# A PSUM tile of its own for the chain of partial results in the FFN pairs with seven products

## The chip, the cores and the metric

The kernel runs on one core of a Trainium2 chip, in one launch. The metric is the device time of that core in microseconds. Before the change it is 1598.57 us, the median of three runs (1598.28 to 1598.74).

## What is computed

One layer of a hybrid streaming encoder is run for 256 prompt frames and 64 sample frames, in float32. The two groups share all weights, so the kernel treats them as one block of T = 320 columns. The reference, cut to the layer:

```python
def layer(x, ...):
    xn = rmsnorm(x, norm_mix[l])
    proj = xn @ w_in[l]                      # q, k, v, u, vs, gates
    ...                                      # attention, spatial gate, merge
    h = x + merged @ w_out[l]
    hn = rmsnorm(h, norm_ffn[l])
    gu = hn @ w_gate_up[l]                   # D_MODEL 2048 -> 2 * 5632
    h = h + (jax.nn.silu(gu[..., :D_FF]) * gu[..., D_FF:]) @ w_down[l]
    return h, k, v, vs
```

The change lies in `hn @ w_gate_up`.

## The kernel before

**Numbers.** A float32 operand is split into a high and a low float16 part (`half` for activations at L168, `high` at L373 and `low` at L377 for weights). A product is then three matmuls into the same PSUM columns: high by high, high by low, low by high (`product`, L104 to L110).

**Tiling.** The FFN has 44 column blocks of 128 features in gate and 44 in up. One group handles a block's gate (unit 0) and its up (unit 1), with 16 blocks along D_MODEL. In an ordinary group (`Group.block`) each unit is 16 times `product`, 48 matmuls of 128x320, into one `acc` tile. ScalarE reads that tile afterwards, in `gated` at L1173 and L1175.

**Pairs with seven products.** In 28 groups (class `Fast`, called pairs here) only high by high is done over all of D_MODEL and all 320 columns (`whole`, L419, 16 matmuls of 128x320 for each unit). The two correction terms are done together for gate and up and for both halves of the columns (N = 160) by a scheme of seven half-size products instead of eight (`cross`, L425, each 16 matmuls of 128x160). It needs four sums of weight parts (`sum_up`, L415, VectorE) and mixed activations (`mix`, made once). In the order in which TensorE does them in a pair, with the tile before the change:

| step | matmuls | tile |
|---|---|---|
| chain, first product (factor 11) | 16 of 160 columns | `more`, columns 0 to 159 |
| whole gate | 16 of 320 | `gate` |
| whole up | 16 of 320 | `up` |
| product 4 | 16 of 160 | `up` |
| chain, second product (factor 2) | 16 of 160 | `more`, columns 0 to 159 |
| product 21 | 16 of 160 | `gate` |
| other (factor 1, with the first sum), first half | 8 of 160 | `more`, columns 160 to 319 |
| row spread for a later group's scale (L222) | 1 of 128 | `row` |
| other, second half | 8 of 160 | `more`, columns 160 to 319 |
| third (factor 3, with the third sum) | 16 of 160 | `more`, columns 320 to 479 |
| product 22 (with the fourth sum) | 16 of 160 | `gate` |

The chain holds partial results that are wanted twice. ScalarE copies it to SBUF after its first product (`seen[:, 0]`, L436) and after its second (`seen[:, 1]`, L437). VectorE puts the pair together in `join` (L457 to L461), one pair later: L457 reads `gate` and `seen`, L458 and L461 read `other`, L459 reads `third`, L460 reads `up`. L1180 multiplies the result, and ScalarE takes its sum of magnitudes (L210).

**Tiles.** A PSUM tile is one bank. `acc` tiles have three banks, `aux` tiles four, `row` one. A new tile takes the bank of that kind that has been free longest, when its first instruction is placed. Before the change a pair takes one `acc` (`gate`) and two `aux` (`up`, `more`). A wait for data or for a bank is kept by whole tile: an instruction that writes into a tile waits for the last reader of it on another engine, whichever columns that reader took.

**Order.** Each engine works through its instructions in the order in which they are written down. Work is written at ticks (`at(tick, fn, rank)`): a pair has four ticks, an ordinary unit two, and what is due at a tick is written in the order of its rank, ahead of the matmuls that follow. A pair's weights are loaded 11 ticks ahead (five `raw` buffers), measured by ScalarE (`bound`, L210), turned into float16 high parts by ScalarE (L375) and low parts by VectorE (L378) into three `w` buffers. L1173 of an ordinary group and L1188 of a down block (`downed`) read a block's `acc` tile one tick after the block has ended. The copies L436 and L437 have rank 0.8 and so come first in their tick; `high` and `gated` have rank 2.

The 28 pairs come in three runs of 8, 12 and 8. In the profile of before they start at 822.97, 1081.89 and 1365.16 us. An ordinary up group stands ahead of the first run, down blocks ahead of the two others.

Of the kernel before, what the change touches and what calls it, by code (L numbers as in the profile page):

```python
# [51 lines left out]
def stream_step(ctx: ExitStack, tc: tile.TileContext, xT, w_in, w_a, w_b, w_out, w_gu, w_down,  # L52
# [10 lines left out]
    def acc():  # L63
        return psum.tile([P, 512], F32, tag="acc", bufs=3, name="acc")

    def aux():
        return psum.tile([P, 512], F32, tag="aux", bufs=4, name="aux")
# [8 lines left out]
    def at(tick, fn, *a, rank=5):  # L76
        if tick <= state["tick"]:
            fn(*a)
        else:
            later.setdefault(tick, []).append((rank, fn, a))  # L80

    def tick():
        state["tick"] += 1
        for _, fn, a in sorted(later.pop(state["tick"], ()), key=lambda x: x[0]):
            fn(*a)
# [305 lines left out]
    class Fast(Group):  # L391
# [35 lines left out]

        def blocks(self, x):
            assert state["tick"] == self.start
            gate, up, more = acc(), aux(), aux()  # L430
            part = lambda ps, n: ps[:, n * N : (n + 1) * N]
            turn_of["seen"] = turn_of.get("seen", 0) + 1
            self.seen = tmp.tile([P, 2, N], F32, tag="seen" if turn_of["seen"] % 2 else "sq", bufs=1, name="seen")
            self.chain, self.other, self.third = (part(more, n) for n in range(3))
            w0, w1, s, mid = self.w[0][2], self.w[1][2], self.sums, HALF // 2
            at(self.start + 1, lambda: nc.scalar.copy(out=self.seen[:, 0], in_=self.chain), rank=0.8)  # L436
            at(self.start + 3, lambda: nc.scalar.copy(out=self.seen[:, 1], in_=self.chain), rank=0.8)  # L437
            self.cross(self.chain, w0, 0, x, 11, start=True, stop=True)
            self.whole(gate, 0, x)
            tick()  # L440
            self.whole(up, 1, x)
            self.cross(part(up, 0), w1, HALF, x, 4, stop=True)
            self.cross(self.chain, s[2], 0, x, 2, stop=True)
            tick()
            self.cross(part(gate, 0), w0, HALF, x, 21)
            self.cross(self.other, s[1], 0, x, 1, range(0, mid), start=True)
            tick()
            self.cross(self.other, s[1], 0, x, 1, range(mid, HALF), stop=True)
            self.cross(self.third, s[3], 0, x, 3, start=True, stop=True)
            self.cross(part(gate, 1), s[4], 0, x, 22, stop=True)  # L450
            tick()
            return gate[:, :T], up[:, :T]
# [41 lines left out]
    first = [[acc(), acc()], [aux(), aux()], [aux(), aux()]]  # L494
# [429 lines left out]
    gate = {}  # L924
# [168 lines left out]
    for made, (kind, s, i) in enumerate(order):  # L1093
        s0, n = SLICES[s]
# [271 lines left out]
```

## Time and profile before

| | |
|---|---|
| median of three runs | 1598.57 us (1598.28 to 1598.74) |
| the profiled execution | 1598.67 us |
| its span, first to last instruction | 1596.9 us |
| TensorE (PE) busy | 1570.6 us, 98% of the span |
| VectorE (DVE) busy | 1214.8 us, 76% |
| ScalarE (ACT) busy | 1115.0 us, 70% |
| granted TensorE clock | 0.998 |
| weights and other data read | 256.03 MB, at 164 GB/s over the span |

A row of the timeline has the start in us, the duration in us, the engine, the line, the operation, the tiles written and read, the shape, and how many such instructions the row holds; in brackets stands how long the engine was idle just ahead of it and what ended that. PE is TensorE's matmul, PEld its weight load. Matmuls are pipelined: a row's duration runs to the modelled end of its last matmul, so the next row starts a little ahead of that end. A row of the groups of lines ends with the idle time ahead of those instructions and what released them. In the chain of waits each share is a part of the span.

### The profile page before, as it was taken

What the parts mean: (1) busy time and instruction counts of PE and PEld (TensorE: products, weight loads), DVE (VectorE), ACT (ScalarE), POOL (GpSimd) and SP (SyncE); (2) the same over time, 40 slices, a digit from 0 to 9 for tenths busy, and PEclk for the clock granted to TensorE, in tenths of its full rate; (3) what the DMA queues carried; (4) which work ended last, traced back from release to release, by engine and by line L of the source; (5) the groups of instructions that cost most, each with busy time, mean ns of one, the idle gap of its engine ahead of it and who ended that gap; (6) DMA issues with size and microseconds to landing.
All of it is one profiled execution on the core that took longest, in us unless ns stands there. A gap on an engine that the chain in (4) does not pass through costs nothing.

```text
span 1596.9 us, 31274 instructions
## 1 busy us (share of the span) xinstructions
PE 1570.6 (98%) x13047; PEld 1244.0 (78%) x13047; DVE 1214.8 (76%) x2109; ACT 1115.0 (70%) x1319; POOL 67.8 (4%) x80
## 2 busy tenths in 40 slices
PE   9999999999999999999999999999999999999997
PEld 9987777777777768879778877778888777888775
DVE  7789887977777766966969956549999655898675
ACT  6589888867556654846777778666777875677663
POOL 0110111100000000121000000000000000000000
PEclk9999999999999999999999999999999999999999
DMA  8567765654444444554554454543444544444441
GB/s 304 200 201 220 198 173 147 190 167 159 159 159 158 160 141 162 185 178 167 187 183 159 160 166 159 167 169 137 180 171 159 174 161 158 159 159 166 125 133 67
DMA packets 92462, 268.55 MB, mean 168 GB/s; under 512 B 28096, under 2 KB 34496, under 8 KB 85152
## 3 DMA queue, kind: packets, MB, share of 16 engines
q1 hardware_dynamic: 89872, 261.36, 49.3%
q0 software_dynamic: 1312, 3.80, 0.7%
q8 instruction: 102, 1.67, 0.4%
q10 hardware_dynamic: 1136, 1.39, 0.3%
q14 instruction: 40, 0.33, 0.1%
HBM read 256.03 MB, written 5.51 MB: 164 GB/s over the span
## 4 chain that ended last, share of the span: by engine, by line
PE 90%; ACT 6%; DVE 3%; issue 2%; DMA 0%; POOL 0%; DVEq 0%; ACTq 0%
PE acc L108 21%; PE acc L110 21%; PE acc L109 21%; PE aux L425 10%; PE acc L425 4%; PE aux L419 4%; PE acc L419 4%; PE aux L541 2%; ACT w L375 1%; PE acc L541 1%; DVE w L378 1%; ACT junk L210 1%; DVE tops L206 1%; ACT seen L437 1%; PE row L222 0%
## 5 line engine op out<-in xcount | busy, mean ns | idle before, releaser
L110 PE MATMUL acc<-half,w 128*128 128x320 f16 x2496 | 746.3, 299 | 1.2 <-DVE w L378 1.1
L108 PE MATMUL acc<-half,w 128*128 128x320 f16 x2496 | 746.4, 299 | 0.4 <-DVE gate L1056 0.3
L109 PE MATMUL acc<-half,w 128*128 128x320 f16 x2496 | 746.3, 299 | 0.0
L375 ACT ACTIVATE w<-raw,up 128x2048 f16<-128x2048 f32 (+1 forms) x216 | 425.1, 1969 | 274.6 <-PE acc L110 172.4
L378 DVE SCALAR_TENSOR_TENSOR w<-raw,up,w 128x2048 f16<-128x2048 f32 (+1 forms) x216 | 499.0, 2311 | 112.1 <-ACT w L375 111.8
L210 ACT ACTIVATE junk<-raw 128x2048 uint8<-128x2048 f32 (+1 forms) x190 | 354.6, 1866 | 6.7 <-issue 1.7
L108 PEld LDWEIGHTS <-w 128*128 128x128 f16 x2496 | 244.2, 98 | 97.6 <-issue 3.0
L110 PEld LDWEIGHTS <-w 128*128 128x128 f16 x2496 | 244.2, 98 | 96.5 <-DVE w L378 1.8
L109 PEld LDWEIGHTS <-w 128*128 128x128 f16 x2496 | 244.2, 98 | 90.8 <-issue 0.9
L226 DVE TENSOR_REDUCE peak<-row 128x1 f32<-128x128 f32 x159 | 45.7, 287 | 127.9 <-PE row L222 127.9
L425 PEld LDWEIGHTS <-sum 128*128 128x128 f16 x1792 | 126.9, 98 | 12.9 <-issue 12.9
L425 PE MATMUL aux<-mix,sum 128*128 128x160 f16 x1344 | 106.6, 232 | 9.4 <-ACT seen L437 9.4
L419 PEld LDWEIGHTS <-w 128*128 128x128 f16 x896 | 86.9, 98 | 31.9
L425 PEld LDWEIGHTS <-w 128*128 128x128 f16 x1344 | 96.2, 98 | 2.4
L415 DVE TENSOR_TENSOR sum<-w,sum 128x2048 f16<-128x2048 f16 x56 | 68.4, 1221 | 2.7
L415 DVE TENSOR_TENSOR sum<-w 128x2048 f16<-128x2048 f16 x56 | 68.2, 1217 | 0.0
L130 ACT CAST w<-raw 128x1024 fp32r<-128x1024 f32 x36 | 37.6, 1045 | 43.3 <-PE acc L110 29.5
L419 PE MATMUL acc<-half,w 128*128 128x320 f16 x448 | 65.4, 299 | 0.0
L419 PE MATMUL aux<-half,w 128*128 128x320 f16 x448 | 65.4, 299 | 0.0
L206 DVE TENSOR_REDUCE tops<-raw 128x1 f32<-128x2048 f32 x26 | 59.2, 2277 | 0.0
L210 ACT ACTIVATE junk<-act 128x320 uint8<-128x320 f32 x42 | 19.6, 467 | 50.4 <-DVE act L1180 41.5
L133 DVE TENSOR_TENSOR w<-raw,w 128x1024 fp32r<-128x1024 f32 x36 | 44.4, 1236 | 5.3 <-ACT w L130 5.2
(258 smaller groups left out, 1716.6 us busy)
## 6 DMA issues: line engine op xcount, KB each, us to landing
raw<-w_in SPq DMA_DIRECT2D x141, 512.0 KB, 4.8
raw<-w_gu SPq DMA_DIRECT2D x56, 1024.0 KB, 4.8
raw<-w_down SPq DMA_DIRECT2D x80, 512.0 KB, 4.0
raw<-w_gu SPq DMA_DIRECT2D x64, 512.0 KB, 4.8
raw<-w_out SPq DMA_DIRECT2D x32, 512.0 KB, 4.9
raw<-w_a SPq DMA_DIRECT2D x16, 512.0 KB, 3.5
raw<-w_b SPq DMA_DIRECT2D x16, 512.0 KB, 4.4
raw<-w_down SPq DMA_DIRECT2D x16, 256.0 KB, 4.1
```

The lines of the kernel that those rows point to most:

```text
L108: nc.tensor.matmul(ps[:, :T], a, x[0], start=first, stop=False, skip_group_check=True)
L109: nc.tensor.matmul(ps[:, :T], a, x[1], start=False, stop=False, skip_group_check=True)
L110: nc.tensor.matmul(ps[:, :T], b, x[0], start=False, stop=last, skip_group_check=True)
L206: nc.vector.tensor_reduce(out=self.tops[:, i : i + 1], in_=src, axis=mybir.AxisListType.X, op=ALU.max, apply_absolute_value=True)
L210: nc.scalar.activation(out=junk, in_=src, func=AF.Abs, accum_out=self.tops[:, i : i + 1])
L226: nc.vector.tensor_reduce(out=top, in_=self.row[:, :P], axis=mybir.AxisListType.X, op=ALU.max)
L375: nc.scalar.activation(out=w[:, 0], in_=self.raw[u][:, : self.width[u]], func=AF.Copy, scale=self.scale.up)
L378: nc.vector.scalar_tensor_tensor(out=self.w[u][1], in0=self.raw.pop(u)[:, : self.width[u]], scalar=self.scale.up, in1=self.w[u][0], op0=AL ...
L415: nc.vector.tensor_tensor(out=self.sums[i], in0=a, in1=b, op=ALU.add)
L419: nc.tensor.matmul(ps[:, :T], self.w[u][0][:, k * P : (k + 1) * P], x.half[k][0], start=k == 0, stop=False, skip_group_check=True)
L425: nc.tensor.matmul(out, w[:, h, (j + k) * P : (j + k + 1) * P], x.mixed[t, k][1 - h], start=start and k + h == 0, stop=stop and k + h == H ...
L541: nc.tensor.matmul(first[b][h][:, :T], w[:, (h * n + j) * P : (h * n + j + 1) * P], xs[c + j][i], start=not last and c + j + i == 0, stop= ...
```

## The change

The chain moves to a tile `first` of its own, of the kind `acc`. `other` and `third` stay in `more`, and move to its first and second 160 columns. No instruction is added or removed. A pair now takes two `acc` tiles and two `aux` tiles.

```diff
-            gate, up, more = acc(), aux(), aux()
+            gate, first, up, more = acc(), acc(), aux(), aux()
...
-            self.chain, self.other, self.third = (part(more, n) for n in range(3))
+            self.chain, self.other, self.third = part(first, 0), part(more, 0), part(more, 1)
```

The order of instructions on every engine stays; the tiles and the waits change. Place 1, on PE in the second pair of the first run, around the row spread between the two halves of `other` (`sum` is the first sum, `mix` the mixed activations, `packed` the operand of the spread). Before:

```order
L425 MATMUL aux_10047<-mix_9414,sum_10040 128x160
L222 LDWEIGHTS packed_10098 [waits DVE_49]
L222 MATMUL row_10180<-turner_91,packed_10098 128x128
L425 LDWEIGHTS sum_10040
L425 MATMUL aux_10047<-mix_9462,sum_10040 128x160 [waits Activation_49]
```

And now:

```order
L425 MATMUL aux_10049<-mix_9414,sum_10041 128x160
L222 LDWEIGHTS packed_10100 [waits DVE_49]
L222 MATMUL row_10182<-turner_91,packed_10100 128x128
L425 LDWEIGHTS sum_10041
L425 MATMUL aux_10049<-mix_9462,sum_10041 128x160
```

The wait of the second half of `other` for ScalarE, whose instruction is the copy L437, is gone.

Place 2, on ACT at the start of the first run. `acc_9717` and `acc_9786` are the gate and up tiles of the ordinary group that ends there, `acc_9652` is the up tile of the group ahead of it, and `acc_9853` is the first pair's `gate` in both programs. Before:

```order
L436 COPY seen_9856<-aux_9855 128x160 [waits PE_49]
L375 ACTIVATE w_9894<-raw_9602,up_9842 128x2048 [waits DVE_49]
L1173 ACTIVATE ev_9896<-acc_9717,undo_9610 128x320
L1175 ACTIVATE bb_9897<-acc_9786,undo_9610 128x320
L375 ACTIVATE w_9957<-raw_9646,up_9842 128x2048 [waits DVE_49,PE_49]
```

And now:

```order
L436 COPY seen_9857<-acc_9854 128x160 [waits PE_49]
L375 ACTIVATE w_9895<-raw_9602,up_9842 128x2048 [waits DVE_49]
L1173 ACTIVATE ev_9897<-acc_9717,undo_9610 128x320
L1175 ACTIVATE bb_9898<-acc_9786,undo_9610 128x320
L375 ACTIVATE w_9958<-raw_9646,up_9842 128x2048 [waits DVE_49,PE_49]
```

The rows stand as before, but the chain is now an `acc` tile, `acc_9854`, and it takes the next bank of that kind: the one of `acc_9652`, which `acc_9853` had before. `acc_9853` goes one further, to the bank of `acc_9717`, and its first matmul waits for L1173, the third row.

Place 3, on PE between the second and the third pair of the first run. Before:

```order
L425 MATMUL acc_10045<-half_9196,sum_10150 128x160
L425 LDWEIGHTS w_10086
L425 MATMUL aux_10243<-half_8913,w_10086 128x160 [waits PE_49]
L425 LDWEIGHTS w_10086 [waits DVE_49]
L425 MATMUL aux_10243<-half_8913,w_10086 128x160
```

And now:

```order
L425 MATMUL acc_10046<-half_9196,sum_10152 128x160
L425 LDWEIGHTS w_10088 [waits Activation_49]
L425 MATMUL acc_10244<-half_8913,w_10088 128x160 [waits PE_49]
L425 LDWEIGHTS w_10088 [waits DVE_49]
L425 MATMUL acc_10244<-half_8913,w_10088 128x160
```

The first matmul of the third pair's chain waits for TensorE's own last product in the first pair's `gate`, whose bank it takes; the two waits at LDWEIGHTS are for the high and low weights. From here on the tiles rotate in this way: a pair's `first` takes the bank of the `gate` of two pairs ago, and its `gate` takes the bank of the last pair's `first`, behind that pair's copy L437.

## The prediction

> **What bounds the kernel now.** I read the chain of waits on the page first, then the groups of lines, then who waited for whom. The rows are the chain's shares by engine, the costliest group of `cross`, and TensorE's longest wait in total.
>
> ```profile
> PE 90%; ACT 6%; DVE 3%; issue 2%; DMA 0%; POOL 0%; DVEq 0%; ACTq 0%
> ...
> L425 PE MATMUL aux<-mix,sum 128*128 128x160 f16 x1344 | 106.6, 232 | 9.4 <-ACT seen L437 9.4
> ...
> PE aux L425 <- ACT seen L437: 9.4, 28, 0.4
> ```
>
> TensorE is the path, and its largest wait is the one that the change aims at: 28 times, once a pair, some 0.33 us for the copy L437. How that looks in a pair shows the timeline of the third pair of the first run, TensorE's rows and the copy.
>
> ```profile
> 854.79 1.27 PE L425 MATMUL aux<-mix,sum 128*128 128x160 f16 x16
> 855.90 1.27 PE L425 MATMUL acc<-half,w 128*128 128x160 f16 x16
> 857.01 0.72 PE L425 MATMUL aux<-mix,sum 128*128 128x160 f16 x8
> 857.56 0.22 PE L222 MATMUL row<-turner,packed 128*128 128x128 bf16 x1
> 857.76 0.29 ACT L437 COPY seen<-aux 128x160 f32<-128x160 f32 x1 [0.76 <-PE aux L425]
> 858.11 1.82 PE L425 MATMUL aux<-mix,sum 128*128 128x160 f16 x24 [0.33 <-ACT seen L437]
> 859.76 1.27 PE L425 MATMUL acc<-half,sum 128*128 128x160 f16 x16
> 860.87 1.27 PE L425 MATMUL aux<-half,w 128*128 128x160 f16 x16
> ```
>
> The chain's second product runs from 854.79 and is done by 856.06. The copy starts only at 857.76, when the first half of `other` (857.01, the same tile) has ended at 857.73, and the second half waits for the copy in turn. Two engines take turns at one tile, for columns that don't overlap.
>
> **What the removed wait is worth.** The idle time in brackets is counted from a modelled end; what is lost is the delay of the next start. For that I need the start after a row spread where nothing waits, and the same wait in the last two pairs of a run, which have no spread at that place.
>
> ```profile
> 920.23 0.72 PE L425 MATMUL aux<-mix,sum 128*128 128x160 f16 x8
> 921.33 1.82 PE L425 MATMUL aux<-mix,sum 128*128 128x160 f16 x24 [0.38 <-ACT seen L437]
> ...
> 924.09 0.22 PE L222 MATMUL row<-turner,packed 128*128 128x128 bf16 x1
> 924.14 0.30 PE L108 MATMUL acc<-half,w 128*128 128x320 f16 x1
> ```
>
> A spread holds up the next start by 924.14 - 924.09 = 0.05 us. So in a pair the second half could start at 857.61 and starts at 858.11: **0.50 us**. Without a spread, eight matmuls take 857.56 - 857.01 = 0.55 us, so 920.78 against 921.33: **0.55 us**. A run has two such pairs. Runs of 8, 12 and 8 pairs save 6 x 0.50 + 2 x 0.55 = 4.1, then 10 x 0.50 + 1.1 = 6.1, then 4.1 us: **14.3 us** in all. The lower bound is the idle time alone, 9.4 us. I take 14.3, as starts are recorded and ends modelled.
>
> **What it adds: a wait at the start of the first run.** There the first pair's `gate` takes the bank that L1173 reads (place 2 above). The rows of before at that place:
>
> ```profile
> 824.08 2.34 PE L419 MATMUL acc<-half,w 128*128 128x320 f16 x16
> 824.28 0.29 ACT L436 COPY seen<-aux 128x160 f32<-128x160 f32 x1 [1.16 <-PE aux L425]
> 824.47 2.01 ACT L375 ACTIVATE w<-raw,up 128x2048 f16<-128x2048 f32 x1
> 826.37 0.52 ACT L1173 ACTIVATE ev<-acc,undo 128x320 f32<-128x320 f32 x1
> ```
>
> L1173 stands on ACT behind the copy L436, which waits for the chain's first product and starts as soon as that has ended, and behind a 2 us conversion. It ends at 826.89. TensorE starts some 0.06 us after ACT ends (L437: 857.76 + 0.29 = 858.05, then 858.11), so at 826.95 and not at 824.08: **2.87 us**, all of it lost, since behind that matmul on PE stands the rest of the pair. L436 is already ahead, so nothing turns in a circle. The bounds are 0, if the bank were free, and 2.87. I take 2.87.
>
> At the start of the other runs a down block's L1188 on VectorE frees the bank. The rows are of the second run and of the third.
>
> ```profile
> 1079.82 0.55 DVE L1188 SCALAR_TENSOR_TENSOR h<-acc,undo,h 128x320 f32<-128x320 f32 x1
> 1083.00 2.34 PE L419 MATMUL acc<-half,w 128*128 128x320 f16 x16
> ...
> 1363.09 0.55 DVE L1188 SCALAR_TENSOR_TENSOR h<-acc,undo,h 128x320 f32<-128x320 f32 x1
> 1366.27 2.34 PE L419 MATMUL acc<-half,w 128*128 128x320 f16 x16
> ```
>
> It ends at 1080.37 and 1363.64, 2.6 us early in both: no cost. In all later pairs `gate` waits for the last pair's copy L437, done some 4 us before: no cost either.
>
> **What is late next: VectorE, through ScalarE.** A pair takes TensorE 12.63 us now (860.87 - 848.24 below) and 12.13 without the wait. Can VectorE follow? Its rows in the same pair, with ScalarE's conversions:
>
> ```profile
> 848.24 1.27 PE L425 MATMUL aux<-half,w 128*128 128x160 f16 x16
> 851.44 0.48 DVE L457 TENSOR_TENSOR ev<-acc,seen 128x320 f32<-128x320 f32 x1
> ...
> 853.56 1.22 DVE L415 TENSOR_TENSOR sum<-w,sum 128x2048 f16<-128x2048 f16 x1
> 854.70 4.69 DVE L378 SCALAR_TENSOR_TENSOR w<-raw,up,w 128x2048 f16<-128x2048 f32 x2
> 855.00 2.00 ACT L375 ACTIVATE w<-raw,up 128x2048 f16<-128x2048 f32 x1 [0.52 <-PE aux L425]
> 859.30 0.55 DVE L1180 SCALAR_TENSOR_TENSOR act<-bb,undo,ev 128x320 f32<-128x320 f32 x1
> ...
> 864.08 0.48 DVE L457 TENSOR_TENSOR ev<-acc,seen 128x320 f32<-128x320 f32 x1
> ```
>
> From L457 to L457 it is 12.64 us as well, and VectorE hardly rests: its one wait is at the second L378. That ends at 859.39 and lasts 2.35, so it starts at 857.04, right behind the conversion that ends at 857.00. The first L378 would have let it start at about 854.70 + 2.35 - 0.09 = 856.96 (the next instruction starts 0.09 ahead of an end, 859.30 against 859.39). So VectorE's own pace is 12.63 - 0.08 = **12.55 us**, and TensorE would draw away by 0.42 us in each pair until something VectorE feeds comes too late.
>
> What comes first is no product of VectorE but the copy L436. ScalarE waits for L1180, then takes three sums of magnitudes, then does the copy, and the chain's second product waits for it.
>
> ```profile
> 847.31 0.47 ACT L210 ACTIVATE junk<-act 128x320 uint8<-128x320 f32 x1 [1.89 <-DVE act L1180]
> 851.85 0.27 ACT L436 COPY seen<-aux 128x160 f32<-128x160 f32 x1
> ...
> 1110.77 0.27 ACT L436 COPY seen<-aux 128x160 f32<-128x160 f32 x1
> 1113.72 1.27 PE L425 MATMUL aux<-mix,sum 128*128 128x160 f16 x16
> ...
> 1199.20 0.27 ACT L436 COPY seen<-aux 128x160 f32<-128x160 f32 x1
> 1209.80 0.28 ACT L436 COPY seen<-aux 128x160 f32<-128x160 f32 x1
> ```
>
> In the third pair of the second run it ends at 1111.04, so the product could start at 1111.10 and starts at 1113.72: 2.62 us to spare, the same in every pair up to the tenth. The eleventh copy comes 10.60 us behind the tenth instead of 12.63, so the last two pairs have 2.03 us more. At pair k TensorE is ahead of before by 0.50 (k - 1), VectorE and ScalarE by 0.08 (k - 2). In the **second run** pair 7 just passes (3.00 against 2.62 + 0.40), pair 8 waits 0.40 us, pairs 9 and 10 0.42 each: **1.24 us** given back. In the third run the last such pair is the sixth (2.50 against 2.94): nothing. In the first the wait of 2.87 us lets the others catch up: nothing.
>
> The end of the second run has little room too: low weights of the next group, ready at 1229.42, are wanted by the third matmul at 1233.88.
>
> ```profile
> 1227.07 2.35 DVE L378 SCALAR_TENSOR_TENSOR w<-raw,up,w 128x2048 f16<-128x2048 f32 x1
> 1233.88 0.30 PE L110 MATMUL acc<-half,w 128*128 128x320 f16 x1
> ```
>
> 4.46 us to spare, TensorE 4.9 earlier, VectorE 0.7: it just holds. Behind it the copy L437 no longer holds up ScalarE.
>
> **The sum.** First run 4.1 - 2.87 = 1.2, second 6.1 - 1.24 = 4.9, third 4.1: **10.2 us**. From the profiled execution's 1598.67 us that gives 1588.5. The median of the runs is 0.1 us lower, so the forecast is **1588.4 us**, 0.64% faster.
>
> **The rivals.**
> - *VectorE binds sooner.* For it speaks that it is busy nearly all of a pair; against it the 2.62 us. With half of that, 1.31, the runs would lose 0.4, 2.55 and 0.9 us instead of 1.24 in all: 1591.0 us. With none they would lose 1.7, 3.9 and 2.2: 1594.9 us. Near it lies the case that only the idle 9.4 us return, with no catching up then: 1598.6 - 9.4 + 2.9 = 1592.1 us.
> - *The first pair doesn't wait*, or the wait is caught up: 1598.6 - 14.3 + 1.2 = 1585.5 us. The rows above speak against it.
> - *The wait stays*, because the copy is late for another reason. Then only the new wait is left: 1601.5 us. Against it: the copy's idle time ends with TensorE in the row of 857.76, and ScalarE is free from 857.00 on.
> - *The clock drops in the new gap.* TensorE would idle for 2.87 us, longer than anywhere in the profile; the longest gap, and the granted clock behind it, are these (row of a stretch: from and to, length, busy us of each engine, clock, DMA share, GB/s).
>
> ```profile
> 180.94 0.85 PE L719 MATMUL aux<-S 128*128 128x320 f32 x4 [1.65 <-DVE S L706]
> 181.00:190.00 9.00, 9.00 (x68) 6.92 (x69) 7.48 (x21) 5.82 (x9) 0.54 (x1) 1.00 0.89 269
> ```
>
> A gap of 1.65 us left the clock at 1.00. If 2.87 us halved it for the rest of that pair, some 11.0 us of matmuls (12.13 - 1.11), those would take 11 us more: 1599.4 us. [...]
> - *Slower: a pair waits for the join of the last one.* If `first` took the bank of the last pair's `gate`, each pair would start behind L457, which ends at 851.92 where TensorE is ready at 848.24: 3.74 us with the 0.06, in 25 pairs, 93 us, less what it saves elsewhere: about 1680 us. It decides as soon as fewer than three `acc` banks turn over between two pairs. Place 3 speaks against it: the bank is that of the pair before, long read.
>
> **How the numbers follow.** Forecast 0.66; VectorE sooner or idle time only 0.16; no wait in the first pair 0.08; clock 0.04; the wait stays 0.03; slower by the join 0.03. The range reaches to 1585.2 below (no wait in the first pair) and to 1592.6 above (half the room, or idle time only); beyond it lie 0.15 or so. About 0.2%, 3.2 us, is what a measurement of this kernel can tell from no change. Faster by more (under 1595.4): 0.91, the first three cases and a little more than their 0.90; within: 0.06, mostly the clock and the wait that stays; slower: 0.03.
>
> **What would show it.** In the changed kernel's profile TensorE has no wait for L437. It has one wait of about 2.8 us at L419 for L1173 near 824 us, and in the second run some three waits at L425 for L436, together about 1.2 us. The spacing of pairs falls from 12.63 to 12.13 us, and to about 12.55 in pairs 8 to 10 of that run. Waits for L378 or L415 inside a run, or pairs of 12.55 from the first, would prove the first rival; a clock under 1.00 behind 824 us the fourth.

## The result, and the profile after

The changed kernel takes **1588.48 us** (median of four executions, 1588.21 to 1589.87), against 1598.64 us (1598.28 to 1598.74) of the kernel before on the same chip: a ratio of 0.9939 [0.9921, 0.9956]. The forecast was 1588.4 us. The profiled execution took 1588.39 us with a span of 1586.6 us, which is 10.3 us less than before, at the same clock of 0.998. Times are medians of all executions of a kernel; the profiled one of the kernel with the first pair's old tiles, below, took 4234.56 us, so no row of it is used.

From the page of the changed kernel: the engines' totals, the chain's shares, and two groups of lines; the last row is the second group in the kernel before.

```profile
PE 1566.6 (99%) x13047; PEld 1242.7 (78%) x13047; DVE 1212.0 (76%) x2109; ACT 1110.1 (70%) x1319; POOL 67.8 (4%) x80
...
PE 81%; DVE 9%; ACT 6%; issue 3%; DMA 1%; DVEq 0%; POOL 0%; ACTq 0%; SPq 0%
...
L425 PE MATMUL aux<-mix,sum 128*128 128x160 f16 x896 | 67.8, 233 | 0.0
...
L210 ACT ACTIVATE junk<-act 128x320 uint8<-128x320 f32 x42 | 19.6, 468 | 81.3 <-DVE act L1180 72.1
```

```profile
L210 ACT ACTIVATE junk<-act 128x320 uint8<-128x320 f32 x42 | 19.6, 467 | 50.4 <-DVE act L1180 41.5
```

The engines' counts of instructions are those of before. The group of `cross` that idled for 9.4 us before idles for 0.0 now; it has 896 matmuls instead of 1344, as the chain's second product now writes an `acc` tile and stands in a group of its own. Two shifts say what has moved closer to the end: the chain runs through VectorE for 9% of the span where it was 3%, and ScalarE waits 72.1 us for L1180 where it waited 41.5. That is VectorE setting ScalarE's pace.

Whom TensorE waits for, in total, times and longest, from the view of waits over the whole span:

```profile
PE acc L419 <- ACT ev L1173: 2.7, 1, 2.7
PE row L222 <- DVE peak L226: 2.4, 6, 0.5
...
PE acc L425 <- ACT seen L436: 0.2, 1, 0.2
```

The 28 waits for L437 are gone. The one long wait for L1173 is there, and of the expected three waits for L436 the view lists one. (L226 stood there before, with the same 2.4 us.)

The start of the first run, from the timeline of ScalarE and TensorE:

```profile
822.85 1.27 PE L425 MATMUL acc<-half,w 128*128 128x160 f16 x16
824.16 0.29 ACT L436 COPY seen<-acc 128x160 f32<-128x160 f32 x1 [1.16 <-PE acc L425]
824.35 2.00 ACT L375 ACTIVATE w<-raw,up 128x2048 f16<-128x2048 f32 x1
826.25 0.52 ACT L1173 ACTIVATE ev<-acc,undo 128x320 f32<-128x320 f32 x1
826.82 2.33 PE L419 MATMUL acc<-half,w 128*128 128x320 f16 x16 [2.70 <-ACT ev L1173]
```

TensorE's order is as it was, yet the whole gate starts 0.05 us behind the end of L1173 (826.77), which has a copy and a 2.00 us conversion ahead of it on ScalarE.

Then the pairs. The first two rows are the starts of the third and fourth pair of the first run; the rest is from the second run, from its tenth pair on: starts of the chain, two copies L436, and the wait of the tenth chain's second product.

```profile
850.01 1.27 PE L425 MATMUL acc<-half,w 128*128 128x160 f16 x16
862.16 1.27 PE L425 MATMUL acc<-half,w 128*128 128x160 f16 x16
...
1184.32 0.27 ACT L436 COPY seen<-acc 128x160 f32<-128x160 f32 x1
1190.23 1.27 PE L425 MATMUL acc<-half,w 128*128 128x160 f16 x16
1196.87 0.27 ACT L436 COPY seen<-acc 128x160 f32<-128x160 f32 x1
1197.19 1.27 PE L425 MATMUL acc<-mix,sum 128*128 128x160 f16 x16 [0.24 <-ACT seen L436]
1202.78 1.27 PE L425 MATMUL acc<-half,w 128*128 128x160 f16 x16
1214.92 1.27 PE L425 MATMUL acc<-half,w 128*128 128x160 f16 x16
```

A free pair, one in which TensorE waits for nothing, takes 12.15 us (862.16 - 850.01; over the seven starts from 837.86 to 910.75 us 12.148), where before it took 12.63. The copies L436 come every 12.55 us (1196.87 - 1184.32), which is VectorE's pace as forecast. The tenth pair takes 12.55 us as well (1202.78 - 1190.23): there TensorE has caught up with that pace. The eleventh is free again, 12.14 us.

Last, the end of the second run: the spread L222, its operand from VectorE, and the next group's first matmul, after and then before.

```profile
1227.01 0.16 DVE L218 TENSOR_SCALAR packed<-topmost 128x1 bf16<-128x1 f32 x1
1227.22 0.10 PEld L222 LDWEIGHTS <-packed 128*128 128x128 bf16 x1 [0.24 <-DVE packed L218]
1227.29 0.30 PE L108 MATMUL acc<-half,w 128*128 128x320 f16 x1
```

```profile
1220.92 1.27 PE L425 MATMUL aux<-half,w 128*128 128x160 f16 x16
...
1229.52 0.16 DVE L218 TENSOR_SCALAR packed<-topmost 128x1 bf16<-128x1 f32 x1
...
1233.55 0.22 PE L222 MATMUL row<-turner,packed 128*128 128x128 bf16 x1
1233.60 0.30 PE L108 MATMUL acc<-half,w 128*128 128x320 f16 x1
```

The last pair took 12.68 us before (1233.60 - 1220.92) and takes 12.37 now (1227.29 - 1214.92). That is 0.31 us less, not the 0.54 of the eleventh (12.68 to 12.14): the spread waits some 0.22 us for L218. The trace shows this wait in the weight load's row, not in the view of TensorE's waits.

### The profile page after: what moved, and what is told of

It reads as the page before. It is cut to its first block, busy times and chain, and to the rows that moved or that the text cites. A ratio compares the mean times of both kernels' runs of the same rounds, so it can differ in the third digit from the quotient of the medians.

```text
span 1586.6 us, 31277 instructions
## 1 busy us (share of the span) xinstructions
PE 1566.6 (99%) x13047; PEld 1242.7 (78%) x13047; DVE 1212.0 (76%) x2109; ACT 1110.1 (70%) x1319; POOL 67.8 (4%) x80
## 4 chain that ended last, share of the span: by engine, by line
PE 81%; DVE 9%; ACT 6%; issue 3%; DMA 1%; DVEq 0%; POOL 0%; ACTq 0%; SPq 0%
PE acc L108 21%; PE acc L109 21%; PE acc L110 21%; PE acc L425 5%; PE aux L425 4%; DVE w L378 3%; PE acc L419 3%; PE aux L419 3%; ACT w L375 2%; PE aux L541 2%; DVE sum L415 1%; ACT junk L210 1%; PE acc L541 1%; DVE tops L206 1%; PE row L222 1%
## 5 line engine op out<-in xcount | busy, mean ns | idle before, releaser
L375 ACT ACTIVATE w<-raw,up 128x2048 f16<-128x2048 f32 (+1 forms) x216 | 424.9, 1968 | 263.1 <-PE acc L110 170.3
L378 DVE SCALAR_TENSOR_TENSOR w<-raw,up,w 128x2048 f16<-128x2048 f32 (+1 forms) x216 | 497.5, 2310 | 105.6 <-ACT w L375 105.1
L226 DVE TENSOR_REDUCE peak<-row 128x1 f32<-128x128 f32 x159 | 45.5, 286 | 127.0 <-PE row L222 127.0
L210 ACT ACTIVATE junk<-act 128x320 uint8<-128x320 f32 x42 | 19.6, 468 | 81.3 <-DVE act L1180 72.1
L425 PE MATMUL acc<-half,w 128*128 128x160 f16 x896 | 71.1, 233 | 0.0
L415 DVE TENSOR_TENSOR sum<-w,sum 128x2048 f16<-128x2048 f16 x56 | 68.3, 1220 | 2.7
L415 DVE TENSOR_TENSOR sum<-w 128x2048 f16<-128x2048 f16 x56 | 68.1, 1216 | 0.0
L425 PE MATMUL aux<-mix,sum 128*128 128x160 f16 x896 | 67.8, 233 | 0.0
```

Of the source, the lines that this page charges most:

```text
L210: nc.scalar.activation(out=junk, in_=src, func=AF.Abs, accum_out=self.tops[:, i : i + 1])
L226: nc.vector.tensor_reduce(out=top, in_=self.row[:, :P], axis=mybir.AxisListType.X, op=ALU.max)
L375: nc.scalar.activation(out=w[:, 0], in_=self.raw[u][:, : self.width[u]], func=AF.Copy, scale=self.scale.up)
L378: nc.vector.scalar_tensor_tensor(out=self.w[u][1], in0=self.raw.pop(u)[:, : self.width[u]], scalar=self.scale.up, in1=self.w[u][0], op0=AL ...
L415: nc.vector.tensor_tensor(out=self.sums[i], in0=a, in1=b, op=ALU.add)
L425: nc.tensor.matmul(out, w[:, h, (j + k) * P : (j + k + 1) * P], x.mixed[t, k][1 - h], start=start and k + h == 0, stop=stop and k + h == H ...
```

## The experiments

The theory is that of the prediction: a wait of about half a microsecond goes in each of 28 pairs, one of 2.87 us comes at the first run's start through the bank of `gate`, and VectorE's pace, by way of ScalarE's copy L436, takes back some in the second run alone. All ratios are against the kernel before, run beside it on the same chip. Its medians there were 1598.55 us for the first four and 1598.57 us for the rest. Diffs are against the changed kernel.

**The first pair with the old tiles.** If the new wait is the price of the bank that `gate` takes there, it goes when that pair alone keeps the old tiles.

```diff
-            gate, first, up, more = acc(), acc(), aux(), aux()
+            gate, up, more = acc(), aux(), aux()
+            old = not turn_of.get("seen")
...
-            self.chain, self.other, self.third = part(first, 0), part(more, 0), part(more, 1)
+            self.chain, self.other, self.third = [part(more, n) for n in range(3)] if old else [part(t, n) for t, n in ((acc(), 0), (more, 0), (more, 1))]
```

> The changed kernel, but the first pair of the first run keeps the chain in the tile of the other products, as before the change. Theory (the new wait of 2.87 us at L419 for L1173 is lost in full, and comes from the bank that gate takes): that wait goes, this one pair keeps its old 0.50 us, so 1588.5 - 2.87 + 0.50 = 1586.1 us, with one wait for the second copy left. Rival (the wait is caught up later, since VectorE and ScalarE use it to run ahead): no gain, 1588.5 to 1589.0 us.

Measured: 1585.97 us, ratio 0.9921 [0.9905, 0.9938]. That is 2.51 us less than the change, or 2.42 when each is set against the kernel before beside it. It is near 2.86 - 0.49 = 2.37, since this pair still pays its old wait. The wait of the first pair costs what the rows say, and nothing behind it catches it up.

**The kinds exchanged: the chain in an `aux` tile, the products in an `acc` tile.** The first pair's `gate` keeps its old bank, and the chain has its own tile in all 28 pairs.

```diff
-            gate, first, up, more = acc(), acc(), aux(), aux()
+            gate, first, up, more = acc(), aux(), aux(), acc()
```

> The changed kernel with the two kinds swapped: the chain has an aux tile of its own, the other products share an acc tile. gate then takes the bank that it took before the change, and the acc tile that is new is first written two thirds into the pair. Theory: all 28 waits for the second copy stay away, the wait for L1173 goes as well, 1588.5 - 2.87 = 1585.6 us. Rival (the new acc tile waits for the join of the last pair, L457, in every pair): waits at L425 for L457, up to 25 of them, and a time above 1588.5 us.

Measured: **1585.48 us** (1585.40 to 1585.59), ratio 0.9918 [0.9902, 0.9935]. The next two kernels come within 0.1 us of it, and these three are the fastest here. TensorE has no wait for L457, on which the rival rested. Its timeline at the first run's start:

```profile
822.85 1.27 PE L425 MATMUL aux<-half,w 128*128 128x160 f16 x16
823.96 2.34 PE L419 MATMUL acc<-half,w 128*128 128x320 f16 x16
```

The whole gate starts at 823.96 instead of 826.82: the wait cost 2.86 us. The first run now gains 3.98 us (the second starts at 1077.79), where the change gained 1.12.

**The cause without a new tile.** The old tiles stay, but the second copy reads what the first one has written to SBUF, and so no longer reads the tile that TensorE goes on writing.

```diff
-            gate, first, up, more = acc(), acc(), aux(), aux()
+            gate, up, more = acc(), aux(), aux()
...
-            self.chain, self.other, self.third = part(first, 0), part(more, 0), part(more, 1)
+            self.chain, self.other, self.third = (part(more, n) for n in range(3))
...
-            at(self.start + 3, lambda: nc.scalar.copy(out=self.seen[:, 1], in_=self.chain), rank=0.8)
+            at(self.start + 3, lambda: nc.scalar.copy(out=self.seen[:, 1], in_=self.seen[:, 0]), rank=0.8)
```

> The kernel before the change; the second copy of the chain (L437) reads the first copy in SBUF and no longer the tile in PSUM, so up and the second half of gate lack the chain's second product. ScalarE does as much as before, no tile and no bank changes. Theory (each pair loses the delay of the next start, 0.50 to 0.55 us): 14.3 us less, some 0.7 us given back in the second run, 1585.0 us (1584.5 to 1585.6). Rival (only the idle time that the profile shows is lost): 1598.6 - 9.4 = 1589.2 us.

Measured: 1585.57 us, ratio 0.9919 [0.9904, 0.9934], within 0.1 us of the kernel with the kinds exchanged. A tile of its own isn't what makes the pair shorter. What counts is that no late reading of the tile stands between two of its writers. The change gets there with a tile apart, which the runs put at 0.485 us in 22 of the pairs and 0.54 in six.

**The reading of the ordinary group first.** The tiles of the change, with L1173 and L1175 ahead of the copy L436 and the conversion at the first run's start.

```diff
-            at(state["tick"] + 1, gated, s, pg, pu, g, rank=2)
+            at(state["tick"] + 1, gated, s, pg, pu, g, rank=0.7 if s == 0 and i == FAST[0][0] - 1 else 2)
```

> The changed kernel; where the first pair follows an ordinary group, that group's read-out (L1173, L1175) stands on ScalarE ahead of the chain's first copy and the 2 us conversion, not behind them. Same tiles and banks as the changed kernel. Theory (the wait comes from the place of L1173 on ScalarE): L1173 ends before 824.0 us, the wait at L419 goes, 1585.6 us. Rival (the wait is for something else that came last): a wait of over 1 us stays at L419 and the time stays above 1587.5 us.

Measured: 1585.58 us, ratio 0.9919 [0.9904, 0.9934], 2.90 us less than the change. L1173 now ends at 823.20 us, and no wait for it is left. The same wait goes in another way, by order instead of by tile. So it is L1173's place on ScalarE that costs, not the number of `acc` banks as such.

**VectorE made slower.** Two small copies more in each `join`, in the kernel with the kinds exchanged. If VectorE's pace is the next bound, they cost time though they stand on an engine that is idle for a quarter of the span.

```diff
+    spare = const.tile([P, 1], F32, name="spare")
...
+            for _ in range(2):
+                nc.vector.tensor_copy(spare, eps_t)
```

> The kernel with the kinds swapped (1585.5 us), with two VectorE copies of 128x1 added at the end of each join, some 0.36 us a pair, that nothing waits for. Theory (behind the removed wait VectorE's own pace, 12.55 us a pair, is next, and it reaches TensorE through L1180 and the copy L436): pace 12.9 us, TensorE draws away by some 0.76 us a pair, so waits at L425 for L436 begin some pairs earlier, in all three runs, and the time grows by 3 to 4.5 us, to 1588.5 to 1590.0 us. Rival (VectorE has room, ScalarE's own work sets the copy): at most 0.3 us more, 1585.8 us.

Measured: 1590.40 us, ratio 0.9946 [0.9931, 0.9962], 4.92 us more than without them. Lines from `spare` on stand one further here, so L426 is `cross`, L437 the first copy and L219 `packed`. The added copies as a group of lines:

```profile
L464 DVE COPY spare<-eps_t 128x1 f32<-128x1 f32 x56 | 8.4, 150 | 1.0
```

Waits from 815 to 1530 us of TensorE's matmuls for the copy and of its weight loads for `packed`, and two of the chain's second products in the timeline:

```profile
PE aux L426 <- ACT seen L437: 2.0, 4, 0.5
...
PEld L223 <- DVE packed L219: 3.1, 6, 0.7
```

```profile
1184.66 1.27 PE L426 MATMUL aux<-mix,sum 128*128 128x160 f16 x16 [0.49 <-ACT seen L437]
1197.46 1.27 PE L426 MATMUL aux<-mix,sum 128*128 128x160 f16 x16 [0.49 <-ACT seen L437]
```

The copies L437 come 12.80 us apart (1107.53, 1120.33, 1133.13 us), 0.25 more than before the two were added. TensorE waits for them 0.49 us at a time, the same chain of causes as in the change, only sooner: pairs 7 to 10 of the second run take 12.80 us each. In two points the expectation was wrong. It had these waits in all three runs; the runs of eight pairs have none, as their room lasts through the sixth pair and grows behind it. And these waits are the smaller part: the four pairs lose 4 x 0.65 = 2.6 us where 0.7 was lost without the added copies, so 1.9 of the 4.92 us. The other 3.0 lie at the ends of all three runs (1.0 in the first), where the spread's weight load waits for `packed`: six times, 3.1 us, against one wait of 0.27 without the copies. That put the time slightly above the upper end that was expected.

**The third sum on GpSimd.** Also on the kernel with the kinds exchanged: GpSimd works 4% of the span, and VectorE's pace would fall well below TensorE's.

```diff
-            nc.vector.tensor_tensor(out=self.sums[i], in0=a, in1=b, op=ALU.add)
+            (nc.gpsimd if i == 3 else nc.vector).tensor_tensor(out=self.sums[i], in0=a, in1=b, op=ALU.add)
```

> The kernel with the kinds swapped (1585.5 us), with the third sum of a pair (one of four L415, 1.2 us on VectorE) on GpSimd. Theory: VectorE's pace falls to some 11.4 us, below TensorE's 12.15, so the waits at L425 for L436 in the second run go: 0.65 us less, 1584.9 us. Rival (GpSimd is slow at this or slows VectorE beside it): the third product waits for its sum or VectorE's groups take longer, and the time stays at 1585.5 us or above.

Measured: 1646.86 us, ratio 1.0301 [1.0282, 1.0319]. The theory failed, and the rival's second case came true: GpSimd slows VectorE beside it. The timeline shows the start of a pair, around the addition on GpSimd:

```profile
908.74 4.24 POOL L415 TENSOR_TENSOR sum<-w 128x2048 f16<-128x2048 f16 x1 [10.72 <-DVE w L378]
908.98 0.28 DVE L226 TENSOR_REDUCE peak<-row 128x1 f32<-128x128 f32 x1
...
909.30 3.70 DVE L227 TENSOR_TENSOR down<-peak,bits 128x1 int32<-128x1 int32 x1
...
913.23 2.00 ACT L375 ACTIVATE w<-raw,up 128x2048 f16<-128x2048 f32 x1 [1.29 <-DVE up L228]
...
915.84 1.77 PE L425 MATMUL aux<-mix,sum 128*128 128x160 f16 x16 [2.64 <-DVE sum L415]
```

L227 works on one element a partition, and stands for 3.70 us, where it took 0.16 us in the mean before: it ends at 913.00, as GpSimd's addition does (912.98). The conversion L375 waits for the scale that comes from it, the low weights and the sums follow, and TensorE waits 2.64 us for a sum. In all it waits so 22 times, 42.8 us. In each of the 28 pairs one VectorE instruction beside GpSimd's addition took about as long as the addition had left, or longer: L227 25 times (3.53 to 3.99 us, its end within 0.03 us of the addition's), and three times an L415 (5.08 us instead of 1.22). L226, which in the rows above starts 0.24 us behind the addition, kept to its 0.28 us. Why the ones are slowed and the other isn't is left open here.

The 42.8 us are not the whole loss of 61.4 us. Behind eight of the waits TensorE ran slower for a while: 16 matmuls of 160 columns from 917.40 us took 2.34 us instead of 1.27. The rows are stretches behind the wait that ended at 915.84 us, with the granted clock in the third column from the right; it was 0.50 for the 3.30 us of the first and 1.00 again from 920.00:

```profile
916.50:919.80 3.30, 3.30 (x28) 3.30 (x25) 3.23 (x6) 3.23 (x4) 0.00 (x0) 0.50 0.00 0
920.00:922.00 2.00, 2.00 (x33) 2.00 (x31) 1.97 (x4) 1.10 (x2) 0.00 (x0) 1.00 0.00 0
```

A pair with a wait of 2.64 us took 14.96 us where the clock held (from 891.51 us) and 16.61 where it fell (from 861.57), 1.65 us more; eight times that are 13 us. And a wait costs 0.17 us more than its idle time (2.38 against 2.21 us in the pair from 847.04 us), 4 us in 22 waits. With the 42.8 us that comes to about 60 of the 61.4, as an estimate.

**The exchanged kinds in the second run alone**, the old tiles elsewhere. Does the second run gain by itself what it gained in the whole?

```diff
-            gate, first, up, more = acc(), acc(), aux(), aux()
+            gate, up = acc(), aux()
+            new = 8 <= turn_of.get("seen", 0) < 20
+            first, more = (aux(), acc()) if new else (None, aux())
...
-            self.chain, self.other, self.third = part(first, 0), part(more, 0), part(more, 1)
+            self.chain, self.other, self.third = (part(first, 0), part(more, 0), part(more, 1)) if new else (part(more, n) for n in range(3))
```

> The swapped layout in the 12 pairs of the second run alone, the old layout in the 16 others. Theory (each run's gain is its own, and the second gives 0.65 us back in its pairs 9 and 10): 10 x 0.485 + 2 x 0.54 - 0.65 = 5.3 us, 1593.3 us. Rival (a run's gain is partly taken back behind it, as VectorE is late for the next groups): under 4.8 us, above 1593.8 us.

Measured: 1593.62 us, ratio 0.9969 [0.9957, 0.9981], a gain of 4.95 us, 0.3 less than expected. Waits of TensorE from 815 to 1530 us (L438 and L439 are the two copies here):

```profile
PE aux L425 <- ACT seen L439: 5.4, 16, 0.4
...
PE aux L425 <- ACT seen L438: 0.2, 1, 0.2
```

Sixteen old waits remain in the other two runs, 5.4 us of idle time, and the second run has its one recorded wait for L436, as in the change. From its start to that of the third run, the second takes 278.29 us here and 278.29 with the exchanged kinds everywhere (283.27 before), so its gain doesn't hang on the other runs. The expectation had counted the pairs alone; the 0.3 us short of it are about the wait for `packed` at the spread that the result's last rows show, 0.3 us in this trace.

## Why the prediction was right, and which terms were off

The three runs, measured by the starts of what follows each of them (for the last, 1466.34 before and 1456.04 after), gained 1.12, 5.07 and 3.99 us; forecast were 1.2, 4.9 and 4.1. The sum is 10.2, and the span fell by 10.3.

- **The removed wait.** Forecast 0.50 us a pair and 0.55 in the last two of a run; measured 12.633 - 12.148 = 0.485 and 12.68 - 12.14 = 0.54. Over 28 pairs that is 22 x 0.485 + 6 x 0.54 = 13.9 us instead of 14.3. It isn't the 9.4 us of recorded idle time: counting from start to start was the right choice, and it decided the forecast more than anything else.
- **The new wait at the first run's start.** Forecast 2.87 us, measured 2.86. Four kernels show it, two with other tiles, one with another order on ScalarE and one without the new tile: in each the time is 2.51 to 3.00 us below the change's. With the measured saving the first run gives 6 x 0.485 + 2 x 0.54 - 2.86 = 1.13. The rival without this wait, 1585.5 us, is exactly what the kernel with the kinds exchanged reaches.
- **No cost at the other starts.** TensorE has no wait for L1188, and the third run gains 6 x 0.485 + 2 x 0.54 = 3.99, all that its pairs can.
- **VectorE's pace next, through L436.** The mechanism and its pace of 12.55 us were right, and so was the place, the second run alone. The slower VectorE shows it from the other side, in the same run. **The size was off**: 1.24 us were to be given back in pairs 8 to 10, and 0.64 were, in pairs 9 and 10 (12.39 - 12.15 and 12.55 - 12.15). The step that failed is the term "VectorE and ScalarE by 0.08 (k - 2)". It takes 0.08 us, VectorE's wait in a later pair, for all that VectorE can gain. But in the second pair of the run VectorE had waited 0.45 us for a conversion before, and that wait is gone with the change (before, then after):

```profile
1103.32 2.35 DVE L378 SCALAR_TENSOR_TENSOR w<-raw,up,w 128x2048 f16<-128x2048 f32 x1 [0.45 <-ACT w L375]
```

```profile
1099.27 4.67 DVE L378 SCALAR_TENSOR_TENSOR w<-raw,up,w 128x2048 f16<-128x2048 f32 x2
```

  So VectorE, and with it ScalarE, gained half a microsecond there: the third copy L436 starts 28.39 us behind the run's start (1109.04 - 1080.65) where it was 28.88 before (1110.77 - 1081.89): 0.49 earlier, not 0.08. The 2.62 us of room thus shrank to 2.1 at the third pair, not to 1.7. TensorE draws away by 0.40 a pair (12.55 - 12.15), so the first wait came a pair later. In pairs 9 and 10 the view of waits has one row, of 0.24 us, for the 0.64 us that are lost.
- **The end of the second run.** "It just holds" looked at the low weights (4.46 us to spare), and the spread ahead of them has less: L218 ended at 1229.68 and the spread started at 1233.55 before, 3.87 us. TensorE comes 10 x 0.485 + 2 x 0.54 - 0.64 = 5.29 us earlier there, L218 only 1.27 (2.51 less the 1.24 by which the run starts earlier). The 4.02 between these use up the 3.87, and the spread waits about 0.2. So the second run gave 5.29 - 0.22 = 5.07. The two misses, 0.6 too much and 0.2 too little given back, and the somewhat smaller saving nearly cancel; that the total came within 0.1 us is in part luck.
- **The clock.** TensorE idled for 2.70 us by the record in the new gap. The stretches around that gap, with the clock in the third column from the right:

```profile
824.00:827.00 3.00, 0.30 (x4) 0.14 (x2) 2.97 (x5) 2.84 (x4) 0.00 (x0) 1.00 0.34 139
827.00:831.00 4.00, 4.00 (x31) 2.89 (x30) 2.15 (x2) 0.19 (x1) 0.00 (x0) 1.00 0.26 70
```

  The clock stayed at 1.00, and the 16 matmuls behind the gap took 2.33 us where they took 2.34 before, so that rival is out in this execution. In the whole trace the clock is below 1.00 only behind the last matmul: 0.50 from 1580.00 us on. But the gap isn't too short for a fall: with the third sum on GpSimd the clock fell behind seven waits of 2.64 or 2.65 us and one of 2.33, and held behind three others of 2.64 or 2.65. The length alone doesn't decide it, and what else does is left open here.

  Another execution of the changed kernel might thus have a fall. By the pairs with GpSimd it would cost some 1.65 us, as an estimate, and not the 11 us of the prediction: no run shows half the clock for the rest of a pair. Whether the slowest of the four, 1589.87 us, had one isn't shown.
- **The other rivals** are out: the wait that stays, VectorE binding from the first pair (no wait for L378 or L415 inside a run), and the wait for the join.

Not tried apart: the 0.22 us at the spread rests on the rows of the trace, on the same wait of 0.27 us with the kinds exchanged, and on its growth when VectorE is slower. Nor did any run show the 0.64 us of the second run come back with a faster VectorE, as the sum on GpSimd slowed it.

## What to carry to other kernels

Here two engines took turns at one PSUM tile for columns that don't overlap. In such a case put what is read in between into a tile apart, and count the gain from start to start rather than by the idle time shown. Whoever adds a tile to a rotation should look at the first use after other work: which bank it shifts onto, and what the last reader of that bank has ahead of it on its engine. Here the kind of tile chosen was worth 3.0 us of 13. Before a saving is summed over a run, the pace of the engine behind is to be compared with the new pace, with its room measured at the first step where it really falls behind.

## What the runs showed of the hardware

An addition of 128x2048 float16 took 1.22 us on VectorE and 4.20 in the mean on GpSimd. In all 28 cases one VectorE instruction beside GpSimd's ended with it or behind it, even one of a single element a partition (0.16 us in the mean before, 3.70 beside it), while L226 kept to its 0.28 us. A wait that the record shows as 0.33 us of idle TensorE cost 0.485 us, since matmuls that follow one another without a wait start before the modelled end of the last (a row of 1.27 us is followed after 1.11). With the third sum on GpSimd TensorE had fourteen gaps between 2.2 and 2.7 us. Behind eight of them, 2.33 to 2.65 us long, the granted clock fell, to 0.50 over the 3.30 us shown of one; behind the six others, and behind the changed kernel's 2.70 us, it held.
